# S5 mixer of a two-layer decoder trunk: every block of the gate product from split weights, and a new order of single steps

## The chip, the cores and the metric

The kernel runs on one core of a Trainium2 chip. A core has five engines that work side by side, each through its own instructions in order: TensorE (PE; its weight loads are listed as PEld), VectorE (DVE), ScalarE (ACT), GpSimd (POOL) and SyncE (SP, which here only issues DMAs). TensorE writes its results into PSUM, eight banks of 128 x 512 float32; VectorE and ScalarE read them there. All other tiles lie in SBUF. The metric is the device time of one execution in microseconds (us).

## The reference

A trunk of two layers on 256 rows of width 1024, all in float32. Each layer adds half a SwiGLU block, a mixer, and half a SwiGLU block again; the mixer of layer 0 is an S5 state-space layer, that of layer 1 block attention.

```python
for layer in range(DEPTH):
    h = h + 0.5 * swiglu(rms_norm(h, ...), w_gate, w_up, w_down)
    h = h + mixer(rms_norm(h, mix_norm[layer]))        # S5 in layer 0
    h = h + 0.5 * swiglu(rms_norm(h, ...), w_gate, w_up, w_down)

def s5_mixer(h, ...):
    u = h @ w_in
    y = scan_over_time(lam, B u) @ C + d_skip * u      # 64 groups of 16 channels, 64 states each
    g = gelu(y)
    g = g * sigmoid(g @ w_glu)
    return g @ w_out
```

The change lies in the S5 mixer, in g @ w_glu and in the order of the steps from u = h @ w_in to the first half of g @ w_out. w_in, w_glu and w_out are 1024 x 1024.

## The kernel before

**Products from split weights.** A product that must hold float32 accuracy is made of three products in the type fp32r: a weight w is split into whi, its fp32r rounding (ScalarE), and wlo, the rest w - whi (VectorE), and the other operand likewise; then hi*hi, hi*lo and lo*hi are added up in PSUM (mm3, L398, and L1092 to L1094).

**The stream of weights.** `Stream` (L37) brings all weights of the kernel, in one order, as units of 1 MB into three raw buffers; unit n is loaded when unit n-3 is freed. `split` (L74) splits half a unit: L86 and L87, or L92 and L93 where a norm's gain is multiplied in, each a ScalarE instruction and then a VectorE instruction. Nine pairs of whi and wlo tiles serve as slots; `release` gives one back. `pump` splits the next half if it has been loaded and a slot is free; `get` splits on the spot what a product needs. Freeing a unit issues the next load on SP.

**Blocks left whole.** `add(..., whole=True)` marks a unit that is not split. With WHOLE = 2 this is the first unit of w_glu, which holds the rows of blocks 0 and 1. For these two blocks `glu` multiplies the raw float32 weight with the float32 tile gf (L1090), where other blocks take the three fp32r products. Their unit stays in its raw buffer until the last step of block 1 frees it (L1098).

**The S5 stage** (`s5`, L962). The channels are eight blocks of 128 (b = 0 to 7). The stage is written out as a plan, a string of words, and `step` (L1117) issues one word after the other; that order is the program order on every engine. The words:

- w0, w256, w512 with .t:k are u = h @ w_in for a range of columns, row half t and input block k; with k = 7 ScalarE scales the sum (L999) and VectorE transposes it into U. PSUM tiles pM, two banks in turn.
- t(b): 32 float32 matmuls (L1009) that spread U into the states, in PSUM: banks A0 to A3 for b < 4, then pM in turn. Each issues the load TA of block b+3 on SP.
- r(b): rotation. Two small ScalarE copies (L1020, L1021), six VectorE instructions with two scans (L1028 to L1033), four of POOL (L1035 to L1038, result hr); for b = 1 to 5 the load TE of block b+2.
- y(b): 48 float32 matmuls (L1052) on U and hr with the table TB, then gelu on ScalarE (yg, L1056) and a transpose on VectorE (gs, L1058); the load TB of block b+3.
- g(b): two transposes on TensorE (L1067); then, for blocks that are not whole, ScalarE's fp32r copy (L1070) and VectorE's rest (L1071) into GT, and for all blocks ScalarE's float32 copy gf (L1072). The three read one PSUM bank. GT lies in the buffer ("xa") that the stage's input X used before.
- u(b):o is one step of the gate product g @ w_glu, block b into output block o (`glu`); its sums lie in banks A0 to A3, two output blocks a bank.
- P is a pump; gelu and sigmoid load the ScalarE table ahead of its use; x is the rest of the stage's input.

After the plan, code with loops issues the steps of blocks 6 and 7, each pair of output blocks followed by `gate(i)`, here a(i): a sigmoid of bank Ai on ScalarE (L1103), the multiply on VectorE (L1105), and the split of the result on both (L1107, L1108). Then the first half of the output product follows (`so`, blocks b = 0 and 1 of its four; o(b):q below, with q = 2t + n): it overwrites bank Aq and takes the output of gate b. so(b) needs the weight unit so(b), split in two halves; two pumps stand behind every two steps, one at the end. `boundary` (L373) then makes blocks 2 and 3 with the additions to h (L371) and the preparation of the next SwiGLU.

Units of w_glu and w_out are called glu0 to glu3 and so0 to so3 below, two blocks each.

Of the kernel before, what the change touches and what calls it, by code (L numbers as in the profile page):

```python
# [120 lines left out]
def trunk_kernel(ctx: ExitStack, tc, x, ffn_norm, ffn_w_gate, ffn_w_up, ffn_w_down, mix_norm,  # L121
# [32 lines left out]

    units = []
    where = {}
    WHOLE = 2
    GAIN = {"f00": None, "f01": 8, "f10": 16, "f11": 24, "s5": 32, "moba": 40}

    def add(key, load, gains=None, whole=False):  # L160
# [118 lines left out]
    st = Stream(nc, units, rp, hp)  # L279
# [20 lines left out]
    XP = [xp]  # L300
# [661 lines left out]
    def s5(nxt, entry):  # L962
        V, P = nc.vector, nc.gpsimd
        HALVES = (slice(0, 64), slice(64, 128))
        wstack = ExitStack()
# [108 lines left out]
        def glu(b, os):  # L1074

            u = where["glu", b // 2]
            g = gf[b // 2][:, b % 2, :]
            if b < WHOLE:
                w = st.raw[u][:, b % 2 * 1024:b % 2 * 1024 + 1024]
            else:  # L1080
                gh, gl = GT["h"][:, b, :], GT["l"][:, b, :]
                wh, wl = st.get(u, b % 2)
            for o in os:
                first, last = b == 0 and o % 2 == 0, b == NB - 1
                if first:
                    acc[o // 2] = psA(o // 2)
                d = acc[o // 2][:, (o % 2) * 256:(o % 2) * 256 + 256]
                c = slice(o * 128, o * 128 + 128)
                if b < WHOLE:
                    mm(d, w[:, c], g, start=first, stop=last, skip_group_check=True)  # L1090
                else:
                    mm(d, wh[:, c], gh, start=first, stop=False, skip_group_check=True)  # L1092
                    mm(d, wh[:, c], gl, start=False, stop=False, skip_group_check=True)
                    mm(d, wl[:, c], gh, start=False, stop=last, skip_group_check=True)  # L1094
                if o == 7 and b >= WHOLE:
                    st.release(u, b % 2)
                elif o == 7 and b % 2:
                    st.free_raw(u)  # L1098

        def gate(i):  # L1100

            sg = fp.tile([128, 2, 256], F32, name="sg", tag="gr", bufs=2)
            nc.scalar.activation(sg, acc[i].rearrange("p (a c) -> p a c", a=2), AF.Sigmoid)  # L1103
            g = gf[i]
            V.tensor_tensor(g, g, sg, op=OP.mult)  # L1105
            gh, gl = (GT[p][:, 2 * i:2 * i + 2, :] for p in "hl")
            nc.scalar.activation(gh, g, AF.Copy)  # L1107
            V.tensor_tensor(gl, g, gh.bitcast(F32), op=OP.subtract)  # L1108
# [8 lines left out]
        def step(word):  # L1117
            name, _, ks = word.partition(":")
            ks = [int(k) for k in ks.split("-")] if ks else []
            ks = range(ks[0], ks[-1] + 1) if ks else ()  # L1120
            if name[0] == "w":
                c0, t = name[1:].split(".")
                for k in ks:
                    w_in(int(c0), int(t), k)
            elif name[0] == "u":
                glu(int(name[1]), ks)
            elif name == "x":
                if entry:
# [8 lines left out]
        plan = """
            w0.0:0-1 P x w0.0:2-5 P w0.0:6 w0.1:0 w0.0:7 w0.1:1-4 P w0.1:5-7 w256.0:0-4 w256.1:0-1 t0 w256.0:5  # L1140
            w256.1:2 P w256.0:6 r0 w256.1:3 w256.0:7 P t1 w512.0:0 w256.1:4-7 w512.0:1 r1 w512.0:2-3 t2 gelu
            r2 t3 y0 w512.0:4-5 w512.1:0-1 w512.0:6 w512.1:2 r3 w512.1:3-4 w512.0:7 w512.1:5 y1 w512.1:6-7 g0
            y2 P P u0:0-1 g1 t4 u0:2-3 r4 g2 u0:4 t5 u0:5-7 r5 u1:0 t6 y3 u1:1-2 r6 u1:3-7 u2:0-2 t7 y4 g3
            u2:3-5 r7 y5 u2:6-7 u3:0-2 y6 g4 u3:3-4 g5 u3:5-7 P u4:0 P u4:1 P u4:2 g6 y7 u4:3-4 P P u4:5-7
            u5:0-1 sigmoid g7 u5:2-5 P u5:6-7 P
        """
        for word in plan.split():
            step(word)
        wstack.close()
        lstack.close()  # L1150
        XP[0] = xstack.enter_context(tc.tile_pool(name="xt2", bufs=1))
        for i in range(4):
            glu(6, (2 * i, 2 * i + 1))
            glu(7, (2 * i, 2 * i + 1))
            gate(i)
        for b in range(2):
            for t in range(2):
                for n in range(2):
# [316 lines left out]
```

## Time and profile before

| | |
|---|---|
| median of 3 runs | 982.28 us (981.8 to 982.3) |
| the profiled execution's own time | 982.36 us |
| its span in the trace | 980.4 us |
| first product of the S5 stage (L399 into pM) | 213.48 us |
| first product of o0 | 287.14 us |
| first product of the SwiGLU behind (L553) | 310.77 us |
| DVE / ACT / POOL busy in the span | 70% / 57% / 19% |
| granted clock of TensorE | 0.999 |

Times in a timeline are from the span's start. A row gives start, duration, engine, source line, operation, output <- input, shape, count of merged instructions, and in brackets the idle time ahead with what ended it. TensorE's matmuls are pipelined, so a row's duration includes the pipeline's depth, and what an instruction costs is read from one start to the next. A wait for several semaphores is put down to the one that came last.

### The profile page before, as it was taken

What the parts mean: (1) busy time and instruction counts of PE and PEld (TensorE: products, weight loads), DVE (VectorE), ACT (ScalarE), POOL (GpSimd) and SP (SyncE); (2) the same over time, 40 slices, a digit from 0 to 9 for tenths busy, and PEclk for the clock granted to TensorE, in tenths of its full rate; (3) what the DMA queues carried; (4) which work ended last, traced back from release to release, by engine and by line L of the source; (5) the groups of instructions that cost most, each with busy time, mean ns of one, the idle gap of its engine ahead of it and who ended that gap; (6) DMA issues with size and microseconds to landing.
All of it is one profiled execution on the core that took longest, in us unless ns stands there. A gap on an engine that the chain in (4) does not pass through costs nothing.

```text
span 980.4 us, 17231 instructions
## 1 busy us (share of the span) xinstructions
PE 972.2 (99%) x6727; PEld 867.5 (88%) x6727; DVE 688.8 (70%) x1118; ACT 560.4 (57%) x1008; POOL 186.5 (19%) x364
## 2 busy tenths in 40 slices
PE   9999999999999999999999999999999999999998
PEld 7878888788888999999999999998788899999997
DVE  5799767768768676666667766665789667766662
ACT  7565766553267555555456655544897556655540
POOL 6963544416511000000010000000441010000000
PEclk9999999999999999999999999999999999999999
DMA  8988877887645666565536656562544546656531
GB/s 284 249 269 279 275 261 242 298 324 245 252 173 182 213 208 215 172 212 175 172 125 214 221 173 214 173 215 92 172 145 157 186 143 214 231 174 213 172 130 44
DMA packets 140002, 198.74 MB, mean 203 GB/s; under 512 B 18232, under 2 KB 111504, under 8 KB 139664
## 3 DMA queue, kind: packets, MB, share of 16 engines
q1 hardware_dynamic: 133808, 184.32, 57.5%
q0 software_dynamic: 5536, 12.71, 3.6%
q8 instruction: 53, 0.87, 0.4%
q10 hardware_dynamic: 576, 0.61, 0.3%
q14 instruction: 29, 0.24, 0.1%
HBM read 183.89 MB, written 13.66 MB: 202 GB/s over the span
## 4 chain that ended last, share of the span: by engine, by line
PE 94%; DVE 2%; ACT 2%; issue 1%; POOL 1%; DMA 1%; SPq 0%; POOLq 0%; DVEq 0%; ACTq 0%
PE pM L554 13%; PE pM L553 13%; PE pM L555 13%; PE pA L399 9%; PE pA L401 9%; PE pA L400 9%; PE pM L399 6%; PE pM L400 6%; PE pM L401 6%; PE pA L473 1%; PE pR L1052 1%; PE pR L333 1%; DVE wlo L87 1%; PE pA L1090 1%; PE pR L866 1%
## 5 line engine op out<-in xcount | busy, mean ns | idle before, releaser
L553 PE MATMUL pM<-xa,whi 128*128 128x256 f32 x1056 | 295.7, 280 | 0.0
L554 PE MATMUL pM<-xa,whi 128*128 128x256 f32 x1056 | 294.9, 279 | 0.0
L555 PE MATMUL pM<-xa,wlo 128*128 128x256 f32 x1056 | 294.7, 279 | 0.0
L93 DVE SCALAR_TENSOR_TENSOR wlo<-raw,gT,whi 128x512 fp32r<-128x512 f32 x328 | 228.1, 748 | 71.2 <-ACT whi L92 71.0
L87 DVE TENSOR_TENSOR wlo<-raw,whi 128x1024 fp32r<-128x1024 f32 (+1 forms) x155 | 187.5, 1225 | 56.0 <-ACT whi L86 54.8
L92 ACT ACTIVATE whi<-raw,gT 128x512 fp32r<-128x512 f32 x328 | 213.7, 711 | 16.4 <-PE pA L401 14.6
L554 PEld LDWEIGHTS pM<-xa,whi 128*128 128x128 f32 x1056 | 198.5, 188 | 2.6
L553 PEld LDWEIGHTS pM<-xa,whi 128*128 128x128 f32 x1056 | 198.5, 188 | 2.3
L555 PEld LDWEIGHTS pM<-xa,wlo 128*128 128x128 f32 x1056 | 198.5, 188 | 0.0
L86 ACT ACTIVATE whi<-raw 128x1024 fp32r<-128x1024 f32 (+1 forms) x155 | 158.7, 1049 | 26.1 <-DMA raw<-in_ffn_w_up_dram 9.8
L399 PE MATMUL pA<-whi,ah 128*128 128x512 f32 x352 | 138.8, 394 | 0.0
L400 PE MATMUL pA<-wlo,ah 128*128 128x512 f32 x352 | 137.6, 391 | 0.0
L401 PE MATMUL pA<-whi,al 128*128 128x512 f32 x352 | 137.6, 391 | 0.0
L568 ACT ACTIVATE sg<-gr 128x256 f32<-128x256 f32 x66 | 27.6, 418 | 165.7 <-DVE gr L565 165.7
L399 PE MATMUL pM<-whi,xa 128*128 128x512 f32 (+1 forms) x304 | 122.2, 402 | 0.0
L400 PE MATMUL pM<-wlo,xa 128*128 128x512 f32 (+1 forms) x304 | 115.8, 381 | 0.1
L401 PE MATMUL pM<-whi,xa 128*128 128x512 f32 (+1 forms) x304 | 115.5, 380 | 0.0
L348 POOL TENSOR_TENSOR ms<-ss 128x1 f32<-128x1 f32 x10 | 1.9, 193 | 470.3 <-ACT sq L345 470.3
L401 PEld LDWEIGHTS pA<-whi,al 128*128 128x128 f32 x352 | 66.1, 188 | 14.3
L399 PEld LDWEIGHTS pA<-whi,ah 128*128 128x128 f32 x352 | 66.1, 188 | 11.6
L400 PEld LDWEIGHTS pA<-wlo,ah 128*128 128x128 f32 x352 | 66.2, 188 | 11.3
L565 DVE TENSOR_TENSOR gr<-pM,rrow 128x512 f32<-128x512 f32 x66 | 45.5, 689 | 40.9 <-PE pM L555 40.8
(269 smaller groups left out, 1214.5 us busy)
## 6 DMA issues: line engine op xcount, KB each, us to landing
raw<-in_ffn_w_down_dram SPq DMA_DIRECT2D x44, 1024.0 KB, 5.4
raw<-in_ffn_w_gate_dram SPq DMA_DIRECT2D x80, 512.0 KB, 4.0
raw<-in_ffn_w_up_dram SPq DMA_DIRECT2D x80, 512.0 KB, 5.1
raw<-in_moba_w_qkv_dram SPq DMA_DIRECT2D x12, 1024.0 KB, 5.1
TB<-dB SPq DMA_DIRECT2D x8, 768.0 KB, 6.6
raw<-in_ffn_w_gate_dram SPq DMA_DIRECT2D x16, 256.0 KB, 4.4
raw<-in_ffn_w_up_dram SPq DMA_DIRECT2D x16, 256.0 KB, 4.7
dB<-tt POOLq DMA_DIRECT2D x16, 256.0 KB, 5.1
```

The source lines that it names most:

```text
L86: nc.scalar.activation(hi[:, c], r[:, c], AF.Copy)
L87: nc.vector.tensor_tensor(lo[:, c], r[:, c], hi[:, c].bitcast(F32), op=OP.subtract)
L92: nc.scalar.activation(hi[:, c], r[:, c], AF.Identity, scale=g)
L93: nc.vector.scalar_tensor_tensor(lo[:, c], r[:, c], g, hi[:, c].bitcast(F32), op0=OP.mult, op1=OP.subtract)
L399: mm(o, xh, wh, start=start, stop=False)
L400: mm(o, xh, wl, start=False, stop=False)
L401: mm(o, xl, wh, start=False, stop=stop)
L553: mm(o, a, xh, start=k == 0 and i == 0, stop=False, skip_group_check=True)
L554: mm(o, a, xl, start=False, stop=False, skip_group_check=True)
L555: mm(o, b, xh, start=False, stop=k == 7, skip_group_check=True)
L565: V.tensor_tensor(gr, ps.rearrange("p (i c) -> p i c", i=2), Rr["row"][:, None, :].to_broadcast([128, 2, 256]), op=OP.mult)
L568: nc.scalar.activation(sg, gr[:, 0, :], AF.Silu)
```

## The change

WHOLE becomes 0, so no unit is left whole: glu0 is split in two halves like the others, blocks 0 and 1 of the gate product are made of three fp32r products, and GT is laid out at g(0) instead of g(2). The plan now also holds the steps of blocks 6 and 7, the gates (words a0 to a3) and the first half of the output product (words o0, o1), which the loops issued before; inside it the order of steps and of pumps is new.

```diff
-    WHOLE = 2
+    WHOLE = 0
...
+            elif name[0] == "a":
+                if name == "a0":
+                    wstack.close()
+                    lstack.close()
+                    XP[0] = xstack.enter_context(tc.tile_pool(name="xt2", bufs=1))
+                gate(int(name[1]))
+            elif name[0] == "o":
+                b = int(name[1])
+                for k in ks:
+                    so(b, k // 2, k % 2)
+                    if k == 3:
+                        for i in range(2):
+                            st.release(where["so", b], i)
...
         plan = """
-            w0.0:0-1 P x w0.0:2-5 P w0.0:6 w0.1:0 w0.0:7 w0.1:1-4 P w0.1:5-7 w256.0:0-4 w256.1:0-1 t0 w256.0:5
-            w256.1:2 P w256.0:6 r0 w256.1:3 w256.0:7 P t1 w512.0:0 w256.1:4-7 w512.0:1 r1 w512.0:2-3 t2 gelu
-            r2 t3 y0 w512.0:4-5 w512.1:0-1 w512.0:6 w512.1:2 r3 w512.1:3-4 w512.0:7 w512.1:5 y1 w512.1:6-7 g0
-            y2 P P u0:0-1 g1 t4 u0:2-3 r4 g2 u0:4 t5 u0:5-7 r5 u1:0 t6 y3 u1:1-2 r6 u1:3-7 u2:0-2 t7 y4 g3
-            u2:3-5 r7 y5 u2:6-7 u3:0-2 y6 g4 u3:3-4 g5 u3:5-7 P u4:0 P u4:1 P u4:2 g6 y7 u4:3-4 P P u4:5-7
-            u5:0-1 sigmoid g7 u5:2-5 P u5:6-7 P
+            w0.0:0-1 P x w0.0:2-5 P w0.0:6 w0.1:0 w0.0:7 w0.1:1-5 w256.0:0-1 w0.1:6 P w256.0:2 w0.1:7
+            w256.0:3-4 w256.1:0-2 t0 w256.1:3-4 P r0 w256.1:5 w256.0:5-6 gelu w256.1:6 w256.0:7 t1 w512.0:0 r1
+            w256.1:7 w512.0:1-2 w512.1:0 w512.0:3 P w512.1:1-3 t2 w512.0:4-5 r2 y0 t3 r3 w512.1:4 w512.0:6-7
+            w512.1:5-6 y1 g0 w512.1:7 y2 P u0:0 P u0:1-2 g1 u0:3 g2 u0:4 t4 t5 u0:5 P r4 u0:6-7 y3 u1:0-2 r5
+            u1:3-4 t6 u1:5-7 g3 u2:0-3 r6 u2:4 t7 y4 r7 u2:5-7 y5 g4 u3:0 P u3:1-2 y6 u3:3-4 g5 u3:5-7 u4:0-2
+            P P P g6 u4:3-7 u5:0 y7 u5:1-3 P u5:4-5 g7 u5:6 P u5:7 u6:0 sigmoid u6:1 u7:0-1 a0 u6:2-3 P u7:2-3
+            a1 u6:4-5 u7:4-5 P a2 u6:6-7 u7:6-7 a3 o0:0-1 P P o0:2-3 P P o1:0-1 P P o1:2-3 P
         """
         for word in plan.split():
             step(word)
-        wstack.close()
-        lstack.close()
-        XP[0] = xstack.enter_context(tc.tile_pool(name="xt2", bufs=1))
-        for i in range(4):
-            glu(6, (2 * i, 2 * i + 1))
-            glu(7, (2 * i, 2 * i + 1))
-            gate(i)
-        for b in range(2):
-            for t in range(2):
-                for n in range(2):
-                    so(b, t, n)
-                if t == 1:
-                    for i in range(2):
-                        st.release(where["so", b], i)
-                st.pump(2 - b * t)
```

## The prediction

> **What bounds the kernel now.** I read the page first, then the S5 stage (213 to 311 us) by stretches, then the timeline of each engine there.
>
> ```profile
> PE 972.2 (99%) x6727; PEld 867.5 (88%) x6727; DVE 688.8 (70%) x1118; ACT 560.4 (57%) x1008; POOL 186.5 (19%) x364
> ```
>
> ```profile
> 262.00:282.00 20.00, 18.88 (x288) 17.76 (x282) 12.79 (x21) 11.12 (x22) 7.66 (x9) 1.00 0.60 224
> ```
>
> TensorE is busy for 99% of the span. In 262 to 282 us (columns: length, then busy time of PE, weight load, DVE, ACT, POOL, then clock) it has the stage's largest hole, 1.1 us, at full clock, and VectorE works 12.8 of 20 us. So a TensorE saving counts at once, and so does any lateness of VectorE that outgrows its idle third. These are the TensorE rows I price with:
>
> ```profile
> 241.42 0.34 PE L1052 MATMUL pR<-U,TB 128*64 128x64 f32 x4
> ...
> 242.97 0.50 PE L399 MATMUL pM<-whi,xa 128*128 128x512 f32 x1
> 243.31 0.40 PE L400 MATMUL pM<-wlo,xa 128*128 128x512 f32 x1
> ...
> 244.79 0.34 PE L1052 MATMUL pR<-U,TB 128*64 128x64 f32 x4
> ...
> 253.82 1.15 PE L1009 MATMUL pM<-U,TA 128*64 128x63 f32 x32 [0.33 <-issue]
> 254.77 0.32 PE L1052 MATMUL pR<-U,TB 128*64 128x64 f32 x4
> ...
> 256.30 3.29 PE L1090 MATMUL pA<-gf,raw 128*128 128x256 f32 x14
> ...
> 267.98 0.34 PE L1052 MATMUL pR<-U,TB 128*64 128x64 f32 x4
> ...
> 270.51 0.38 PE L1067 MATMUL pR<-cst,gs 128*128 128x128 f32 x2
> 270.85 0.28 PE L1093 MATMUL pA<-xa,whi 128*128 128x256 f32 x1
> ...
> 278.55 0.41 PE L1067 MATMUL pR<-cst,gs 128*128 128x128 f32 x2 [1.12 <-DVE gs L1058]
> ...
> 282.35 0.28 PE L1094 MATMUL pA<-xa,wlo 128*128 128x256 f32 x1
> 286.91 0.28 PE L1094 MATMUL pA<-xa,wlo 128*128 128x256 f32 x1
> ...
> 288.20 0.40 PE L399 MATMUL pA<-whi,xa 128*128 128x512 f32 x1
> 298.57 0.39 PE L399 MATMUL pA<-whi,xa 128*128 128x512 f32 x1
> ```
>
> Start to start, 39 products of 256 columns take 4.56 us, 0.117 each, so one split gate step (three products) is 0.351. 45 of 512 columns take 10.37, 0.23 each. A y step takes 1.55 to the next product, which is itself 0.11 late (0.34 for 0.23): 1.66. A t step is 0.95, and the way back from it to products 0.23 (1.55 less 48 matmuls at 0.95/32, plus the 0.11). A g step is 0.34 less one product: 0.22.
>
> **The change, part by part.**
>
> *TensorE's work.* Sixteen float32 steps go (seven are the 14 records at 256.30: at most 3.29/7 = 0.47 each; at least 0.42 if the last record's pipeline tail is left out) and sixteen at 0.351 come: -1.1 to -1.9 us, say -1.6. Counting the plan's words, products follow a t or y step 11 times instead of 6; five more returns at 0.23 and entries of some 0.1 are +1.6, from which the changes into and out of float32 that vanish come off (the rows merge them; between 0 and -1.6; I take the middle). Net -0.8, bounds -1.9 to +0.5. The holes of 0.33 (t6) and 1.12 (g7) are there to be won as well.
>
> *VectorE's and ScalarE's work.* Added: two splits of glu unit 0 and, for blocks 0 and 1, the fp32r copy (L1070) and its rest (L1071). L1072's copy reads the same PSUM bank after L1071, so ScalarE, in order, now waits for VectorE in g0 and g1 too; behind g1's wait stand g2's copies, the next split and rotation 4's preparation. The rows that price this:
>
> ```profile
> 246.88 0.45 DVE L1058 STREAM_TRANSPOSE gs<-yg 128x256 f32<-128x256 f32 x1 [0.76 <-ACT yg L1056]
> 247.82 2.36 DVE L87 TENSOR_TENSOR wlo<-raw,whi 128x1024 fp32r<-128x1024 f32 x2 [0.50 <-ACT whi L86]
> 250.10 0.68 DVE L1028 TENSOR_TENSOR wv<-pM,TE 128x512 f32<-128x512 f32 x1
> ...
> 253.63 0.40 DVE L1071 TENSOR_TENSOR xa<-pR,xa 128x256 fp32r<-128x256 f32 x1
> 254.55 0.69 DVE L1028 TENSOR_TENSOR wv<-pM,TE 128x512 f32<-128x512 f32 x1 [0.52 <-ACT pM L1020]
> ...
> 260.77 1.26 DVE L1033 TENSOR_TENSOR_SCAN zo<-rh,pM 128x256 f32<-128x256 f32 x2
> ...
> 270.44 0.40 DVE L1071 TENSOR_TENSOR xa<-pR,xa 128x256 fp32r<-128x256 f32 x1
> 271.57 0.42 DVE L1071 TENSOR_TENSOR xa<-pR,xa 128x256 fp32r<-128x256 f32 x1 [0.73 <-ACT xa L1070]
> 273.40 3.50 DVE L87 TENSOR_TENSOR wlo<-raw,whi 128x1024 fp32r<-128x1024 f32 x3 [1.40 <-ACT whi L86]
> ...
> 265.33 0.74 POOL L1038 TENSOR_TENSOR hr<-pv,pv 128x256 f32<-128x256 f32 x1
> ```
>
> *Up to y2: nothing.* Ahead of y2 stand the same words in both plans (all w, t0 to t3, y0, y1, g0), so I leave y2 at 244.8.
>
> ```profile
> 240.93 0.74 POOL L1038 TENSOR_TENSOR hr<-pv,pv 128x256 f32<-128x256 f32 x1
> ```
>
> A split of glu unit 0 now stands between rotations 1 and 2, 1.2 us (2.1 beside POOL, below). Today POOL is through with rotation 2 at 241.7, y2 needs it at 244.8: 3.1 us of TensorE's steps cover it. Without that cover it would cost its 1.2 to 2.1.
>
> *Rotation 4, then t6.* Today gs2, two subtracts (247.82) and rotation 4 at 250.10. New order: gs2, two subtracts, rest of g1, rest of g2, a third subtract, rotation 4. The pattern rest, rest, subtract stands at 270.44, 271.57, 273.40: 2.96 us, because of ScalarE's hops. Rotation 4 starts at 250.1 + 2.96 + 1.17 = 254.2, ends (3.53, 250.10 to 253.63) at 257.8. t6 takes over t4's PSUM bank and waits for that: 257.95. TensorE is ready earlier: y2 and y3 3.32, 13 gate steps 4.56, g1 and g2 0.44, t4 and t5 2.13: 10.5 behind 244.8, 255.3. **Wait 2.6.**
>
> *Rotation 6, then y6.* 257.8, a transpose 0.4, rotation 5 to 261.7, a rest with its hop 0.92 (253.63 to 254.55), rotation 6 from 262.6 to 266.1; POOL needs 4.05 more (scan's end 262.03 to 266.07): y6 at 270.3, today 267.98. TensorE's own work from t6: t6 and t7 2.36, y4 and y5 3.32, 14 gate steps 4.91, g3 and g4 0.44: 269.0. **Wait 1.3.**
>
> *Up to g7.* 266.1, transpose and rotation 7 to 270.05, transpose, rest of g4 at 270.45; subtract of glu2's first half 1.83 later (271.57 to 273.40), 272.3. POOL is still at rotation 7 then. The one subtract that ran beside POOL's SBUF products:
>
> ```profile
> 227.80 2.09 DVE L87 TENSOR_TENSOR wlo<-raw,whi 128x1024 fp32r<-128x1024 f32 x1
> ...
> 228.77 2.17 POOL L1036 TENSOR_TENSOR pv<-zo,TE 128x512 f32<-128x512 f32 x1
> ```
>
> 2.09 instead of 1.17 (POOL's usual is 1.19): bounds 1.17 and 2.09, I take the latter. Then gs6 and the rest of g5 at 274.8; from there the same chain as today (that rest at 271.57, three splits, rest of g6, gs7) leads to g7 6.98 later: 281.7. TensorE's own work gives 280.9 (today's 9.45 from y6 to the hole before g7, less g4, plus four gate steps).
>
> The Trainium skill ("GPSIMD Engine Reference", 1. Specifications) says that GpSimd shares its SBUF interfaces with VectorE and contends with instructions that have two SBUF inputs. The 2.09 agrees with it, and by it two more splits (glu0's first, glu2's first) run at that price; by a plain 1.17 the end comes 0.8 earlier, 985.7.
>
> *The gates.* The splits of so1 move from ahead of all gates to between them.
>
> ```profile
> 279.83 1.28 ACT L234 ACT_TABLE_LOAD   x1
> ...
> 284.27 0.59 ACT L1103 ACTIVATE sg<-pA 128x512 f32<-128x512 f32 x1
> 286.45 0.63 ACT L1107 ACTIVATE xa<-gf 128x512 fp32r<-128x512 f32 x1 [1.59 <-DVE gf L1105]
> ...
> 285.74 0.68 DVE L1105 TENSOR_TENSOR gf<-gf,sg 128x512 f32<-128x512 f32 x1
> ...
> 287.73 0.68 DVE L1105 TENSOR_TENSOR gf<-gf,sg 128x512 f32<-128x512 f32 x1
> ...
> 291.71 0.68 DVE L1105 TENSOR_TENSOR gf<-gf,sg 128x512 f32<-128x512 f32 x1
> ...
> 294.05 4.63 DVE L87 TENSOR_TENSOR wlo<-raw,whi 128x1024 fp32r<-128x1024 f32 x4 [0.26 <-ACT whi L86]
> ...
> 302.88 0.69 DVE L371 SCALAR_TENSOR_TENSOR h<-pA,h 128x512 f32<-128x512 f32 x1 [0.22 <-PE pA L401]
> ```
>
> Behind g7: the subtract of so0's first half, the rest of g7, copy, the next split, the table load, sigmoid 0: its multiply about 5.2 us after g7, 286.9 (an estimate: subtract with hop 1.5, rest 0.45, copy 0.3, split 0.95, table 1.4, sigmoid 0.6). A gate takes 1.99 from multiply to multiply (285.74, 287.73); with a split behind it, 2.34 to the subtract (291.71 to 294.05) plus 1.17: 3.5. Multiplies at 286.9, 290.4, 293.9. Sigmoid 2 starts 0.71 (285.74 to 286.45) + 0.54 + 0.95 behind multiply 1, ends 293.2; o0:2 overwrites the bank that it reads. TensorE, 281.7 + 0.22 + 18 gate steps + 0.3 (for g7's rest) + 12 products, is there at 291.3: **wait 1.9.** Sigmoid 3 ends at 295.8, **wait 1.2** for o0:3. The 30 products left (o0:3 and o1) end at 302.7; today the products behind them begin at 298.57: **+4.1.**
>
> *Boundary.* The last multiply, 295.9, plus today's 11.2 (291.71 to 302.88) frees VectorE at 307.1; TensorE needs the first sum at 302.7 + 4.31 = 307.0. +0.1; bounds 0 and +1 if the next phase's first load lands later behind its subtract.
>
> *Queues.* SP issues in program order: glu3's megabyte moves ahead of TA7, so0's ahead of TE6, TB6, TE7. I cost that at nothing (rival 4). gelu's table load (1.3) moves ahead of t1, where ScalarE waits for products; if not, it costs 1.3 once. g0 takes over the s5 input's buffer while the last w step has yet to read block 7; g0 writes block 0, so I cost no wait (rival 3).
>
> Sum: 982.36 (the profiled run; the median shown is 982.28) + 4.2 = **986.5 us**; its own range 985.2 to 988.
>
> **The rivals.** 1. *VectorE keeps pace* (the other side). Place: rotation 4 to y6 and the gates. For it: the 7 us idle in 262 to 282, more than the 3.2 added (two subtracts 2.34, two rests 0.8). Against: the order puts the additions ahead of rotation 4. It decides where rotation 4 starts before 251.6 and sigmoid 2 ends before TensorE is at o0:2. Then -0.8 - 0.33 - 1.12: 980.1. 2. *Only the gates wait*, the rotations keep up: 980.1 plus 1.5 for each of the two splits between gates less the 0.3: 982.8. For it: the gates' order is in the plan itself, and the rotations' lateness hangs on ScalarE's hops; against: rotation 4 has three subtracts ahead of it however the hops fall. 3. *A wait for the old buffer*: the last w step waits for g0's copies, about 1.1 (the hop 270.44 to 271.57), carried to the end: 987.6. For it: one buffer, two tiles; against: other blocks. 4. *SP's queue*: so0's load waits for glu1's second subtract (254.2), and TE6 stands behind its issue, say at 254.8.
>
> ```profile
> TE<-dE SPq DMA_DIRECT2D x8, 260.0 KB, 4.5
> ...
> raw<-in_s_w_in_dram SPq DMA_DIRECT2D x1, 1024.0 KB, 14.0
> ```
>
> At 4.5 us TE6 lands at 259.3, rotation 6 needs it at 262.6: 3.3 us of slack, against which stands that a load has taken 14. Half way between, 9.25, it lands at 264.05 and costs 1.5: 988.0.
>
> **How the numbers follow.** Forecast 0.58, rival 1 0.13, rival 2 0.13, rival 3 0.08, rival 4 0.08. About 0.2% (2 us) can be told from no change: faster is below 980.3, slower above 984.2. Faster: rival 1, most of it, 0.13. Same: rival 2, 0.13. Slower: the rest, 0.74. The range leaves out rival 1 and a little above: 981.5 to 988.8.
>
> **What would show it.** No L1090 rows; a hole of about 2.6 us ahead of t6 (L1009), released by VectorE's scan, and 1.3 ahead of y6, released by POOL; rotation 4 near 254; subtracts of about 2 us beside L1035 and L1036; multiplies of L1105 3.5 apart where a split lies between; two holes in the first so products. I am wrong if t6 runs on without a hole, or if the sigmoids stay 2 us apart.

## The result, and the profile after

| | before | after |
|---|---|---|
| median of 6 executions each | 982.28 us (981.8 to 982.86) | 987.31 us (985.8 to 987.91) |
| ratio | | 1.0049 [1.0038, 1.0061] |
| span of the profiled execution | 980.4 us | 985.9 us |
| granted clock of TensorE in the six executions of after | | 0.998, 0.998, 0.998, 0.998, 0.997, 1.0 |

The changed kernel is 5.0 us slower; 986.5 had been forecast. The sixth execution, the only one with the full clock, took 985.8 us. The profiled execution took 987.91 us.

In the trace of after the stage begins 0.74 us later than in that of before, with the same code ahead of it: the rest of the stage's input (L336), at 214.39 us then, stands at 215.13 now. Forecast times below are moved by this 0.74. VectorE's timeline of after (start, duration, engine, line, operation; in brackets the idle time ahead and what ended it):

```profile
215.13 0.69 DVE L336 TENSOR_TENSOR xa<-pR,xa 128x512 fp32r<-128x512 f32 x1 [0.37 <-ACT xa L335]
...
251.32 0.42 DVE L1071 TENSOR_TENSOR xa<-pR,xa 128x256 fp32r<-128x256 f32 x1
252.47 0.42 DVE L1071 TENSOR_TENSOR xa<-pR,xa 128x256 fp32r<-128x256 f32 x1 [0.72 <-ACT xa L1070]
254.29 1.23 DVE L87 TENSOR_TENSOR wlo<-raw,whi 128x1024 fp32r<-128x1024 f32 x1 [1.40 <-ACT whi L86]
255.43 0.68 DVE L1028 TENSOR_TENSOR wv<-pM,TE 128x512 f32<-128x512 f32 x1
...
263.73 0.42 DVE L1071 TENSOR_TENSOR xa<-pR,xa 128x256 fp32r<-128x256 f32 x1 [0.82 <-ACT xa L1070]
264.67 0.69 DVE L1028 TENSOR_TENSOR wv<-pM,TE 128x512 f32<-128x512 f32 x1 [0.52 <-ACT pM L1020]
...
274.20 1.57 DVE L87 TENSOR_TENSOR wlo<-raw,whi 128x1024 fp32r<-128x1024 f32 x1 [1.40 <-ACT whi L86]
...
288.29 0.69 DVE L1105 TENSOR_TENSOR gf<-gf,sg 128x512 f32<-128x512 f32 x1 [0.78 <-ACT sg L1103]
...
291.77 0.68 DVE L1105 TENSOR_TENSOR gf<-gf,sg 128x512 f32<-128x512 f32 x1
...
295.24 0.69 DVE L1105 TENSOR_TENSOR gf<-gf,sg 128x512 f32<-128x512 f32 x1
```

The first block is the forecast pattern word for word: rest, rest, third subtract, and then rotation 4 at 255.43. The multiplies of the gates stand 3.48 apart where a split lies between. TensorE's timeline of after, its rows with idle time, and the first product behind the stage:

```profile
259.15 1.98 PE L1009 MATMUL pM<-U,TA 128*64 128x63 f32 x32 [2.50 <-issue]
...
272.32 0.34 PE L1052 MATMUL pR<-hr,TB 128*64 128x64 f32 x4 [0.18 <-POOL hr L1038]
...
282.98 0.41 PE L1067 MATMUL pR<-cst,gs 128*128 128x128 f32 x2
...
294.60 0.50 PE L399 MATMUL pA<-whi,xa 128*128 128x512 f32 x1 [1.62 <-ACT sg L1103]
297.13 0.50 PE L399 MATMUL pA<-whi,xa 128*128 128x512 f32 x1 [0.86 <-ACT sg L1103]
316.25 0.37 PE L553 MATMUL pM<-xa,whi 128*128 128x256 f32 x1
```

Holes, times in which TensorE is idle, of 2.50 us ahead of t6, 1.62 ahead of o0:2 and 0.86 ahead of o0:3; in y6 next to none (0.18). g7 no longer waits. But t6's 32 matmuls, 1.15 us long before, take 1.98. The busy time by stretches of after says why (length, then busy time of PE, weight load, DVE, ACT, POOL with instruction counts, then granted clock, DMA share, GB/s):

```profile
256.00:258.00 2.00, 0.65 (x6) 0.45 (x4) 1.80 (x5) 0.00 (x0) 0.00 (x0) 1.00 0.71 166
...
259.00:260.00 1.00, 0.84 (x16) 0.88 (x18) 1.00 (x4) 0.00 (x0) 0.81 (x1) 0.57 0.99 379
260.00:261.00 1.00, 1.00 (x22) 0.94 (x18) 0.97 (x2) 0.00 (x0) 1.00 (x2) 0.50 1.19 453
261.00:262.00 1.00, 1.00 (x7) 0.94 (x5) 0.83 (x3) 0.00 (x0) 0.92 (x2) 0.50 0.97 402
262.00:263.00 1.00, 1.00 (x8) 1.00 (x7) 0.91 (x2) 0.00 (x0) 1.00 (x2) 0.72 0.52 185
```

Behind the hole the granted clock falls to half for some 3.4 us. Compared with the full clock, these four microseconds lack 0.43 + 0.50 + 0.50 + 0.28 = 1.7 us of work.

The loss adds up on TensorE. From L336 to the first L553 the stage takes 96.38 us before (214.39 to 310.77) and 101.12 after: 4.74 more. Holes go from 0.33 + 1.12 to 2.50 + 0.18 + 1.62 + 0.86 = 5.16, 3.7 more; the half clock is 1.7; the rest, -0.7, is TensorE's own work, a remainder that was not measured by itself.

### The profile page after: what moved, and what is told of

It is laid out like the page before. It is cut to its first block, busy times and chain, and to the rows that moved or that the text cites. A ratio compares the mean times of both kernels' runs of the same rounds, so it can differ in the third digit from the quotient of the medians.

```text
span 985.9 us, 17272 instructions
## 1 busy us (share of the span) xinstructions
PE 973.3 (99%) x6743; PEld 868.9 (88%) x6743; DVE 693.1 (70%) x1122; ACT 563.5 (57%) x1012; POOL 186.3 (19%) x364
## 4 chain that ended last, share of the span: by engine, by line
PE 87%; DVE 5%; ACT 2%; issue 2%; POOL 2%; DMA 1%; SPq 0%; DVEq 0%; POOLq 0%; ACTq 0%
PE pM L554 13%; PE pM L553 13%; PE pM L555 12%; PE pA L399 9%; PE pA L401 9%; PE pA L400 9%; PE pM L399 5%; PE pM L400 5%; PE pM L401 5%; DVE wlo L87 2%; PE pA L473 1%; ACT whi L86 1%; PE pR L333 1%; POOL qrs L306 1%; PE pR L866 1%
## 5 line engine op out<-in xcount | busy, mean ns | idle before, releaser
L553 PE MATMUL pM<-xa,whi 128*128 128x256 f32 x1056 | 295.7, 280 | 0.0
L555 PE MATMUL pM<-xa,wlo 128*128 128x256 f32 x1056 | 294.6, 279 | 0.0
L87 DVE TENSOR_TENSOR wlo<-raw,whi 128x1024 fp32r<-128x1024 f32 (+1 forms) x157 | 190.7, 1229 | 59.1 <-ACT whi L86 57.9
L553 PEld LDWEIGHTS pM<-xa,whi 128*128 128x128 f32 x1056 | 198.5, 188 | 2.3
L86 ACT ACTIVATE whi<-raw 128x1024 fp32r<-128x1024 f32 (+1 forms) x157 | 161.2, 1049 | 27.1 <-DMA raw<-in_ffn_w_up_dram 9.8
L399 PE MATMUL pA<-whi,ah 128*128 128x512 f32 x352 | 138.8, 394 | 0.0
L401 PE MATMUL pA<-whi,al 128*128 128x512 f32 x352 | 137.6, 391 | 0.0
L399 PE MATMUL pM<-whi,xa 128*128 128x512 f32 (+1 forms) x304 | 122.3, 402 | 0.0
L401 PE MATMUL pM<-whi,xa 128*128 128x512 f32 (+1 forms) x304 | 115.4, 380 | 0.0
L401 PEld LDWEIGHTS pA<-whi,al 128*128 128x128 f32 x352 | 66.1, 188 | 14.3
L399 PEld LDWEIGHTS pA<-whi,ah 128*128 128x128 f32 x352 | 66.1, 188 | 11.6
```

What stands on the lines that cost most here:

```text
L86: nc.scalar.activation(hi[:, c], r[:, c], AF.Copy)
L87: nc.vector.tensor_tensor(lo[:, c], r[:, c], hi[:, c].bitcast(F32), op=OP.subtract)
L399: mm(o, xh, wh, start=start, stop=False)
L401: mm(o, xl, wh, start=False, stop=stop)
L553: mm(o, a, xh, start=k == 0 and i == 0, stop=False, skip_group_check=True)
L555: mm(o, b, xh, start=False, stop=k == 7, skip_group_check=True)
```

## The experiments

Time before is the median of the runs of before on the same chip as each group: 982.63 us for the first four, 982.86 for the next four, 982.73 for the last two. The stage is the time from L336 to the first L553 in the run's trace; before has 96.38 us, after 101.12. Two runs of different groups are better compared by it than by their medians.

| run | median, us | ratio to before | stage, us |
|---|---|---|---|
| third_split_later | 985.86 | 1.0034 [1.0022, 1.0047] | 99.39 |
| gates_free | 988.04 | 1.0055 [1.0041, 1.0069] | 101.95 |
| new_plan_whole2 | 985.61 | 1.0031 [1.0019, 1.0042] | 99.39 |
| filler | 986.3 | 1.0038 [1.0025, 1.0051] | 100.31 |
| gates_only | 983.88 | 1.0011 [1.0002, 1.002] | 97.09 |
| old_order_split | 984.6 | 1.0022 [1.0013, 1.0031] | 97.66 |
| best_order_split | 983.63 | 1.0008 [0.9999, 1.0017] | 96.87 |
| best_order_whole2 | 978.27 | 0.9955 [0.9942, 0.9967] | 92.23 |
| best_order_split2 | 978.92 | 0.9962 [0.9949, 0.9974] | 92.20 |
| split2_order_whole2 | 982.71 | 1.0002 [0.9993, 1.0011] | 96.05 |

**third_split_later.** The changed kernel with one pump moved behind rotation 5.

```diff
-            w512.1:5-6 y1 g0 w512.1:7 y2 P u0:0 P u0:1-2 g1 u0:3 g2 u0:4 t4 t5 u0:5 P r4 u0:6-7 y3 u1:0-2 r5
+            w512.1:5-6 y1 g0 w512.1:7 y2 P u0:0 P u0:1-2 g1 u0:3 g2 u0:4 t4 t5 u0:5 r4 u0:6-7 y3 u1:0-2 r5 P
```

> Changed against the new kernel: the split of glu1's second half stands behind rotation 5 instead of ahead of rotation 4. Theory A (VectorE's whole queue up to rotation 6 is the limit, wherever in it the split stands): rotation 4 starts about 2 us earlier and the hole ahead of t6 shrinks from 2.5 to 0.5 us, so the clock is not throttled behind it; but y6, which waits for rotation 6, starts at most 1 us earlier and gets a hole of about 2 us. Time 986.0 (985.4 to 986.6). Rival B (the hole ahead of t6 costs its own length, and the throttled clock on top): y6 3 to 4 us earlier, time 983.7. Rival C (the throttled clock costs nothing because VectorE is the limit either way): time 987.3 as the new kernel, y6 where it was.

985.86 us: theory A. TensorE's timeline, rows with idle time:

```profile
257.25 1.15 PE L1009 MATMUL pM<-U,TA 128*64 128x63 f32 x32 [0.50 <-issue]
...
270.02 0.34 PE L1052 MATMUL pR<-hr,TB 128*64 128x64 f32 x4 [0.99 <-POOL hr L1037]
270.70 0.34 PE L1052 MATMUL pR<-hr,TB 128*64 128x64 f32 x4 [0.35 <-POOL hr L1038]
```

The hole ahead of t6 falls from 2.50 to 0.50 and t6 takes its 1.15 us again, at full clock. The later rotations become the new wait: y5 and y6 wait for the halves of hr that POOL makes, 0.2 + 0.99 + 0.35 us, where after had 0.18. So of the 2.0 us of hole and 1.7 of clock that are won at t6, 1.4 come back in these waits and 0.6 in places where no wait shows; the stage is 1.7 us shorter, the median 1.45.

**filler.** Ten idle products of the helper `busy` ahead of t6, in a word b10 of the plan; they compute nothing that is used.

```diff
+            elif name[0] == "b":
+                busy(int(name[1:]))
...
-            u1:3-4 t6 u1:5-7 g3 u2:0-3 r6 u2:4 t7 y4 r7 u2:5-7 y5 g4 u3:0 P u3:1-2 y6 u3:3-4 g5 u3:5-7 u4:0-2
+            u1:3-4 b10 t6 u1:5-7 g3 u2:0-3 r6 u2:4 t7 y4 r7 u2:5-7 y5 g4 u3:0 P u3:1-2 y6 u3:3-4 g5 u3:5-7 u4:0-2
```

> Changed against the new kernel: ten float32 products of 128 columns of ones into a spare PSUM tile just ahead of t6, so that TensorE is not idle there; their result is not used. Theory A (the hole lets the clock be throttled to half for some 3 us; by that g3's transposes, the rest of g3 and rotation 6 come late): clock 1.000 in every run, steps of 0.117 behind t6, a hole of about 1.2 us ahead of y6; time 985.8 (985.4 to 986.3), the time of the one run of the new kernel whose clock was 1.000. Rival C (VectorE's queue sets y6 either way): 987.3, y6 where it was.

986.3 us, the upper end of theory A's range: filling the hole with useless work makes the kernel 1.0 us faster. TensorE's timeline:

```profile
256.48 2.40 PE L1370 MATMUL pR<-ones 128*128 128x128 f32 x20
259.14 1.15 PE L1009 MATMUL pM<-U,TA 128*64 128x63 f32 x32 [0.27 <-issue]
```

t6 starts where it started (259.15), but takes 1.15 us instead of 1.98: the time of the hole isn't won, only the clock. Of the 1.7 us, 0.4 come back as longer waits for hr: 0.54 (0.18 in after), where 1.2 had been expected.

**gates_free.** The two splits of so1 stand behind the last gate.

```diff
-            P P P g6 u4:3-7 u5:0 y7 u5:1-3 P u5:4-5 g7 u5:6 P u5:7 u6:0 sigmoid u6:1 u7:0-1 a0 u6:2-3 P u7:2-3
-            a1 u6:4-5 u7:4-5 P a2 u6:6-7 u7:6-7 a3 o0:0-1 P P o0:2-3 P P o1:0-1 P P o1:2-3 P
+            P P P g6 u4:3-7 u5:0 y7 u5:1-3 P u5:4-5 g7 u5:6 P u5:7 u6:0 sigmoid u6:1 u7:0-1 a0 u6:2-3 u7:2-3
+            a1 u6:4-5 u7:4-5 a2 u6:6-7 u7:6-7 a3 P P o0:0-1 P P o0:2-3 P P o1:0-1 P P o1:2-3 P
```

> Changed against the new kernel: the two splits of so1 stand behind the four gates instead of between them. Both theories: the gates' multiplies 2.0 us apart, no hole ahead of o0:2 and o0:3. Theory A (a backlog of VectorE: the splits have to be done before o1 anyway): the holes come back ahead of o1, whose weights are late, about 2 us of the 2.5; time 986.8 (986.3 to 987.2). Rival B (the place between the gates is what costs): the two holes of 1.6 and 0.9 us are won, time 984.8.

988.04 us: no gain, and more than either theory had. The multiplies are 2.0 apart now, and the holes ahead of o0 are gone, but the waits of TensorE name new ones (engine, tile, line <- what: total us, times, longest):

```profile
PE pA L399 <- ACT whi L86: 0.8, 1, 0.8
PE pA L400 <- DVE wlo L87: 0.8, 1, 0.8
```

These are the halves of so1, late for o1. The profiled execution was at half clock behind its hole of 2.50 ahead of t6, too, and fell to half once more behind the two new holes (the clock is the third figure from the end):

```profile
299.00:300.00 1.00, 1.00 (x3) 0.50 (x2) 1.00 (x2) 1.00 (x2) 0.00 (x0) 0.50 0.00 0
300.00:301.00 1.00, 1.00 (x4) 0.78 (x3) 1.00 (x2) 1.00 (x2) 0.00 (x0) 0.50 0.34 49
301.00:302.00 1.00, 1.00 (x4) 0.81 (x3) 1.00 (x2) 0.72 (x1) 0.00 (x0) 0.50 1.02 351
```

With 0.87 and 0.93 in the microseconds at both ends that is 1.7 us again, more than the 0.9 by which the holes behind g7 are shorter (1.58 for 2.48). So this run shows that the splits are late for o1 when they are moved, but not what the gates would gain at full clock; its one execution with a clock of 1.0 took 987.62, and why it is no faster stays open.

**new_plan_whole2.** The new plan with blocks 0 and 1 in float32: the order without the added work.

```diff
-    WHOLE = 0
+    WHOLE = 2
```

> The new order of steps, but blocks 0 and 1 of the gate product in float32 from the raw weight as before. Theory A (the order and the added work share the loss): ahead of rotation 4 the three subtracts stay, the two rests with their hops go, so rotation 4 starts 2 to 3 us earlier, t6's hole is under 0.8 us, no throttled clock; every later split is two halves ahead. Time 984.7 (984.0 to 985.5). Rival B (the added work alone): 982.3, as the old kernel. Rival C (the order alone): 987.3, as the new one.

985.61 us, 0.1 above the range of theory A, by which order and added work share the loss; B and C are further off. VectorE's timeline and TensorE's largest wait:

```profile
286.16 0.69 DVE L1105 TENSOR_TENSOR gf<-gf,sg 128x512 f32<-128x512 f32 x1 [0.78 <-ACT sg L1103]
...
295.10 0.69 DVE L1105 TENSOR_TENSOR gf<-gf,sg 128x512 f32<-128x512 f32 x1
```

```profile
PE pA L399 <- ACT sg L1103: 2.5, 2, 1.6
```

t6 has next to no hole here (0.15 us) and the clock stays at 1.00. The first multiply is 0.4 us later than before (285.74) and the last 3.4 (291.71); as the stage begins 0.4 later in this trace, the first stands where it stood, and the last is 3.0 late. So 3.0 us of the change come with the order alone (the stage has 99.39 for 96.38), most of them as the two holes ahead of o0:2 and o0:3, and 1.7 (99.39 to 101.12) with the added work. That is no more than the half clock behind t6's hole takes, which this run doesn't have; filler, at full clock but with the hole's time still lost, lies 0.9 above this run.

**gates_only.** The kernel of before with the two splits of so1 between the gates, all else untouched.

```diff
-            u5:0-1 sigmoid g7 u5:2-5 P u5:6-7 P
+            u5:0-1 sigmoid g7 u5:2-7
...
             glu(6, (2 * i, 2 * i + 1))
+            if i in (1, 2):
+                st.pump()
             glu(7, (2 * i, 2 * i + 1))
```

> The kernel of before with one part of the change alone: the two splits of so1 leave the plan's last line and stand behind glu(6) of the second and of the third gate. All else is as before. Theory A (a split between two gates delays the next multiply): in the trace of before the multiplies of L1105 stand at 285.74, 287.73, 289.72, 291.71, and the first waits for the two subtracts of 283.46; without them it follows the sigmoid, which ends at 284.9, so it comes 0.8 earlier. Then two spacings of 3.5 (measured in the changed kernel: 288.29, 291.77, 295.24) and one of 2.0: the last multiply at 293.95, 2.2 later than before. TensorE, which is at o0:2 at 290.95, waits for sigmoids 2 and 3 (291.25 and 293.8): 0.3 and 1.2, 1.5 together. Time before plus 1.5 to 2.2: 983.8 to 984.6 us, multiplies 3.5 apart. Theory B (the gates have room for a split in the 0.70 that VectorE waits for ScalarE in each): no later than before, 981.8 to 982.6.

983.88 us, 1.0 more than before: the mechanism is A's, the size is less. VectorE's timeline:

```profile
284.34 0.69 DVE L1105 TENSOR_TENSOR gf<-gf,sg 128x512 f32<-128x512 f32 x1 [1.58 <-ACT sg L1103]
...
287.83 0.69 DVE L1105 TENSOR_TENSOR gf<-gf,sg 128x512 f32<-128x512 f32 x1
...
291.31 0.68 DVE L1105 TENSOR_TENSOR gf<-gf,sg 128x512 f32<-128x512 f32 x1
293.30 0.68 DVE L1105 TENSOR_TENSOR gf<-gf,sg 128x512 f32<-128x512 f32 x1
```

The spacings are 3.49, 3.48 and 1.99 as expected; but the first multiply comes 2.1 us earlier (this trace runs 0.7 late), where 0.8 were expected, since ScalarE's part of the two splits had held up the sigmoid as well (it starts at 284.27 before, right behind them, and at 283.71 here). A split between gates costs little if the work taken from ahead of the gates lets the first one start earlier. In the changed kernel it didn't: g7 came late, and a subtract of so0 (286.29) still stood ahead of the first multiply (288.29).

**old_order_split.** The old plan and gate section with WHOLE = 0, two pumps more.

```diff
-    WHOLE = 2
+    WHOLE = 0
...
-            y2 P P u0:0-1 g1 t4 u0:2-3 r4 g2 u0:4 t5 u0:5-7 r5 u1:0 t6 y3 u1:1-2 r6 u1:3-7 u2:0-2 t7 y4 g3
-            u2:3-5 r7 y5 u2:6-7 u3:0-2 y6 g4 u3:3-4 g5 u3:5-7 P u4:0 P u4:1 P u4:2 g6 y7 u4:3-4 P P u4:5-7
+            y2 P P u0:0-1 g1 t4 u0:2-3 r4 g2 u0:4 t5 u0:5-7 r5 u1:0 t6 y3 u1:1-2 r6 u1:3-7 P u2:0-2 t7 y4 g3
+            u2:3-5 r7 y5 u2:6-7 P u3:0-2 y6 g4 u3:3-4 g5 u3:5-7 P u4:0 P u4:1 P u4:2 g6 y7 u4:3-4 P P u4:5-7
```

> The old plan and the old gate section with WHOLE = 0: all products from split weights, with the two subtracts more that this needs ahead of u2:0 and ahead of u3:0 (the two subtracts behind y2 now split glu unit 0). It is the added work without the new order. Theory A (the order made the loss, the added work can be carried): rotation 4 has the same two subtracts ahead of it as before, and the rest of g0 and of g1 besides, of which that of g1 comes with its hop directly ahead, 0.42 + 0.73; so about 1.1 more than the 0.33 of before at t6. Two subtracts of 1.17 more up to g7, of which the idle time of VectorE in 262 to 282 covers none to all: 0 to 2.3. TensorE's products save 1.1 to 1.9 there. Between 981.5 and 984.2, about 983. Theory B (VectorE's work is the bound wherever it stands): its added work of 2 x 1.17 + 2 x 0.42 = 3.2 and the hops of the two rests, 2 x 0.73, come out whole: 986 to 987. Theory C (the new order was needed for the added work, and is the better home for it): later than the changed kernel, over 987.5.

984.6 us, 1.7 more than before. That lies between A and B, 0.4 above A's range. TensorE's waits:

```profile
PE pM L1009 <- issue: 2.3, 1, 2.3
PE pR L1067 <- DVE gs L1058: 1.7, 1, 1.7
```

The holes are those that the kernel before has already, grown: t6's from 0.33 to 2.25, g7's from 1.12 to 1.70. The trace's stage is 1.3 us longer than before's, at full clock. Six of the eleven executions have a clock of 0.999 or 1.0 and took 984.06 to 984.6; the five at 0.998 took 985.35 to 986.2, so part of the median's 1.7 may be the clock, though no trace shows where. So the loss is a sum: 1.3 to 1.7 for the work, about 3 for the order. Theory C is out: the new order was no better home for it.

**best_order_split and best_order_whole2.** Two plans laid out anew, one for WHOLE = 0, one for WHOLE = 2; of each the part from y1 to the gates:

```diff
+            w512.1:5-6 r3 w512.0:4 w512.1:7 y1 g0 w512.0:5-6 g1 w512.0:7 P y2 t4 r4 u0:0 t5 y3 g2 u0:1-2
+            u1:0-2 u0:3 t6 u1:3 r5 u0:4 g3 u2:0 r6 u0:5 u2:1 y4 t7 u0:6 u3:0 u0:7 u2:2-3 u1:4-5 u3:1-2 u2:4
+            u3:3 r7 P y5 g4 y6 u3:4 u1:6 P u2:5 u3:5 P u4:0-1 u1:7 y7 g5 u4:2 g6 u4:3-4 u5:0 g7 u5:1 P u5:2
+            u2:6 u4:5 P u6:0 P u5:3-4 u2:7 P u6:1-4 u7:0-2 P P u5:5 u3:6 u6:5 u4:6 u7:3 u5:6 sigmoid u3:7
+            u4:7 u6:6 u7:4-5 a0 u5:7 u7:6 a1 a2 u6:7 u7:7 a3 P o0:0-2 P o0:3 o1:0 P P o1:1-3 P P
...
-    WHOLE = 0
+    WHOLE = 2
...
+            w512.1:2-3 r3 w512.0:7 w512.1:4-6 P w512.1:7 u0:0 y1 y2 t4 r4 t5 y3 r5 u0:1-2 g1 g2 u0:3-4 u1:0
+            t6 u1:1-4 u0:5 u1:5 u0:6-7 r6 y4 t7 r7 y5 u1:6-7 g3 g4 u2:0-5 u3:0-1 u2:6 g5 P u4:0 u3:2 y6 P
+            y7 u3:3 u4:1 u2:7 P u5:0 u4:2 g6 g7 u5:1 P u3:4 u5:2 u4:3 u6:0 u5:3 P u4:4 u3:5 u4:5 u7:0 u6:1
+            u5:4 P u6:2 u7:1 sigmoid u5:5 u3:6 u7:2 a0 u4:6 u5:6 u6:3-4 u7:3 u3:7 u4:7 u6:5 u7:4-5 u5:7
+            u6:6 a1 u6:7 P u7:6-7 a2 a3 o0:0-2 P o0:3 P o1:0 P o1:1 P P o1:2-3
```

> The changed kernel (WHOLE = 0, all work of it) with its plan in another order: two subtracts fewer stand ahead of rotation 4 (only one, behind g1, ahead of y2), g2's and g3's rests come behind rotations 4 and 5, t6 stands behind u0 to u1:2, products of u0 to u3 are kept back as cover for the rotations, both splits of so1 stand ahead of the first gate, and the last three gates follow each other with few words between. Theory A (the loss is the order's, the work fits): no hole over 1 us ahead of t6, y6 and g7, and no hole of 1 us in the first output products; what is left is TensorE's saving of 0.8 and the 0.33 and 1.12 of old holes: 980 to 982 us. Theory B (VectorE's added 3.2 us is a backlog that any order carries to the gates): the first multiply of L1105 comes 2 to 3 us later than before, and the time is 984 to 986.

983.63 us, between the theories. It avoids the holes that were forecast for the change and has others. Three single waits, in the timelines of ScalarE, TensorE and VectorE:

```profile
245.75 0.39 ACT L1070 ACTIVATE xa<-pR 128x256 fp32r<-128x256 f32 x1 [2.29 <-PE pM L401]
```

```profile
247.06 0.34 PE L1052 MATMUL pR<-U,TB 128*64 128x64 f32 x4 [1.35 <-ACT gf L1072]
```

```profile
261.28 0.69 DVE L1028 TENSOR_TENSOR wv<-pM,TE 128x512 f32<-128x512 f32 x1 [1.36 <-DMA TE<-dE]
```

g0's copy writes into the buffer that the last w steps read, and waits for the last of them, 2.29 us; y2 needs the bank and waits with it. And rotation 6 waits for its table, whose load was issued behind so0's. The second is rival 4's wait. The first is at rival 3's buffer, but runs the other way: rival 3 let the last w step wait for g0's copies.

> The same step function with a plan laid out anew in the same way, but with blocks 0 and 1 in float32 as before (WHOLE = 2): no work added, order alone. Theory A (the order of before had 0.33 and 1.12 us of holes and VectorE bound the boundary behind the gates; an order can win them): 979 to 981 us, without holes over 0.5 us ahead of t6, y6 and g7. Theory B (TensorE's own work is the bound and the old order already hid all but those holes, each plan has its own returns to pay): 981.5 to 983. If this kernel is faster than best_order_split by 1 us or more, split weights for blocks 0 and 1 are not worth their VectorE work under any of the orders tried; if the two are alike, the choice of weights matters less than the order.

978.27 us, faster than before by 4.6, a little beyond theory A. TensorE's only wait in the stage:

```profile
PE pR L1052 <- POOL hr L1038: 0.3, 1, 0.3
```

Rotations 4 to 7 (247.46 to 260.43 us) run without a split's subtract between them, the next one is at 268.68, and but for one at 284.12 all that so1 needs lie ahead of the gates. So the old order itself left 4.6 us (4.15 of them in the stage), of which only 1.45 showed as holes in its trace. By the measure set beforehand this run, 5.4 us below best_order_split, spoke against the split weights; the next one takes that back.

**best_order_split2 and split2_order_whole2.** One more plan for WHOLE = 0, without the three waits above, and the same plan with WHOLE = 2.

```diff
+            w0.0:0-1 P x w0.0:2-5 P w0.1:0-4 w0.0:6-7 w0.1:5 P w0.1:6 w256.0:0 w0.1:7 w256.0:1 P w256.0:2 P
+            w256.0:3-5 w256.1:0 w256.0:6 w256.1:1 w256.0:7 w256.1:2-3 t0 w256.1:4-5 P w256.1:6 P P w256.1:7
+            t1 w512.0:0 w512.1:0 r0 w512.1:1-3 gelu r1 w512.1:4 t2 w512.1:5 r2 w512.0:1 w512.1:6-7 t3 y0
+            w512.0:2 r3 w512.0:3-7 y1 g0 t4 r4 y2 t5 g1 u0:0 r5 u0:1 y3 u1:0 u0:2 g2 u0:3-4 u1:1-2 u0:5 t6
+            t7 r6 y4 u2:0 g3 u1:3 u2:1 u0:6 u1:4 u2:2-4 r7 y5 g4 u1:5 u3:0-2 y6 g5 u0:7 u3:3 g6 u1:6 u2:5
+            u3:4 u2:6 P u1:7 P y7 u3:5 u2:7 P u4:0-2 u5:0 sigmoid g7 u5:1-2 u6:0 u4:3 P u5:3 P u3:6 u6:1 P
+            u6:2 u4:4 u5:4 u4:5 u7:0-1 u6:3 P P u4:6 u7:2 a0 u6:4 u7:3 P u7:4 u5:5 P u3:7 a1 u5:6 u4:7
+            u6:5-6 u7:5-6 u5:7 u6:7 a2 u7:7 a3 o0:0-3 o1:0-2 P P P P P o1:3
```

> The changed kernel (WHOLE = 0) with one more order, made against what the trace of best_order_split shows: there g0's copy waited for the last w step (y2 behind it 1.35 us late, t4 0.86), and rotation 6 waited 1.36 us for its table, issued behind the load of so0 (y6 behind it 1.3 late). Here g0 stands behind all w steps, rotation 4 follows t4 with no subtract ahead of it but those long done, and the splits of glu 1 to so1 stand behind rotation 7. Theory A (the added work can be carried whole, what is lost in an order are such single waits): the 983.63 of best_order_split less 1.35 + 0.86 and most of 1.3: 980 to 981.5. Theory B (VectorE's added 3.2 us stays as a backlog behind rotation 7 and comes out at the gates in any order): first multiply of L1105 again 1 us or more later than before's 285.74, 983 to 985.

978.92 us: theory A, and faster than its range. All work of the changed kernel is in it, and TensorE has no wait in the stage. VectorE's timeline and one stretch:

```profile
246.92 0.69 DVE L1028 TENSOR_TENSOR wv<-pM,TE 128x512 f32<-128x512 f32 x1 [0.52 <-ACT pM L1020]
...
251.71 0.69 DVE L1028 TENSOR_TENSOR wv<-pM,TE 128x512 f32<-128x512 f32 x1 [0.52 <-ACT pM L1020]
...
256.50 0.69 DVE L1028 TENSOR_TENSOR wv<-pM,TE 128x512 f32<-128x512 f32 x1 [0.52 <-ACT pM L1020]
...
261.30 0.69 DVE L1028 TENSOR_TENSOR wv<-pM,TE 128x512 f32<-128x512 f32 x1 [0.52 <-ACT pM L1020]
...
269.93 2.36 DVE L87 TENSOR_TENSOR wlo<-raw,whi 128x1024 fp32r<-128x1024 f32 x2 [1.40 <-ACT whi L86]
...
281.65 0.68 DVE L1105 TENSOR_TENSOR gf<-gf,sg 128x512 f32<-128x512 f32 x1
...
299.07 0.69 DVE L371 SCALAR_TENSOR_TENSOR h<-pA,h 128x512 f32<-128x512 f32 x1 [3.04 <-PE pA L401]
```

```profile
240.00:256.00 16.00, 16.00 (x308) 14.44 (x308) 13.79 (x27) 4.55 (x14) 12.59 (x15) 1.00 0.86 285
```

Rotation 4 is at 246.92 instead of 255.43, and the four follow each other in 4.8 us with one rest between; no split comes between them. Four subtracts of glu 0 and 1 lie ahead, at 223 to 229 us, where TensorE has w steps; eight lie behind rotation 7. VectorE is busy 13.8 of 16 us in 240 to 256, in after 10.7: the same work, earlier. The first multiply is at 281.65, 4.1 us ahead of before's, and at the boundary it is VectorE that waits for TensorE (3.04 us).

> The order of best_order_split2 with blocks 0 and 1 in float32 (WHOLE = 2): the same order without the added work; the two splits that it doesn't need are done earlier for later units. The pair prices the added work within one order, as the pairs before/old_order_split (1.7) and new_plan_whole2/changed kernel (1.7) do within theirs. Theory A (that price is 1.5 to 2 us in any order, because VectorE has no spare time near the gates): 1.5 to 2 us below best_order_split2. Theory B (in an order laid out for it the added work is covered, and TensorE's saving of 0.8 shows): 0.5 to 1 us above best_order_split2.

982.71 us: neither theory, 3.8 above its twin. Timelines of ScalarE and of TensorE:

```profile
224.79 1.06 ACT L86 ACTIVATE whi<-raw 128x1024 fp32r<-128x1024 f32 x1 [2.03 <-DMA raw<-in_s_w_glu_dram]
...
228.95 2.00 ACT L86 ACTIVATE whi<-raw 128x1024 fp32r<-128x1024 f32 x2 [1.79 <-DMA raw<-in_s_w_glu_dram]
```

```profile
231.37 0.50 PE L399 MATMUL pM<-whi,xa 128*128 128x512 f32 x1 [1.88 <-ACT us L999]
```

With unit glu0 whole, the early pumps split later units, and these haven't landed: ScalarE waits 2.03 and 1.79 us for their loads, the scaling of the w sums (L999) waits behind it, and TensorE 1.88 behind that and 0.54 once more. So this pair doesn't price VectorE's added work; it shows that a plan fits the units that it was laid out for. The remaining 1.4 of the 3.8 are TensorE's own work, added up in the way of the next paragraph: 0.7 in the steps u, 0.55 in the transposes of g, 0.25 in the w and o products, and 0.1 less in t and y.

**The gate product itself.** Adding up, from TensorE's timelines, the time from each start to the next (a hole counts to the row ahead of it) gives for the steps u, split and whole together, and for the w and o products from the stage's first product on:

| | before | after | old_order_split | best_order_whole2 | best_order_split2 | split2_order_whole2 |
|---|---|---|---|---|---|---|
| steps u, us | 27.50 | 28.43 | 28.83 | 24.85 | 24.01 | 24.71 |
| w and o0 to so3 products (L399 to L401), us | 46.09 | 49.14 | 45.89 | 45.17 | 45.70 | 47.83 |
| L336 to first L553, us | 96.38 | 101.12 | 97.66 | 92.23 | 92.20 | 96.05 |

Between the two plans with next to no holes, best_order_whole2 (0.35 us) and best_order_split2 (none), the steps u differ by 0.84 us for the split weights, and the rest by 0.8 against them, 0.53 of it in the w and o products; the stages are equal to 0.03 us, and 978.27 and 978.92 lie 0.07% apart. The two plans differ in more than the weights; within one plan, best_order_split2's, the steps u are 0.7 us shorter with split weights.

## Why the prediction was right

The time (986.5 for 987.31) and the sign are right, and so is the mechanism, VectorE's lateness at rotation 4 and at the gates. That the number is so near is in part luck: a loss that the prediction doesn't have, the half clock, stands in for waits that didn't come, and its times are too short for TensorE's own work.

- **TensorE's work, -0.8.** The sum over the stage leaves -0.7. Right as a term; the forecast's times don't keep to it (see the sum).
- **Up to y2, nothing.** y2 at 245.85, forecast 245.54. Right to 0.3 us; g0's copy did wait 0.67 us for the last w step, and VectorE's rest (L1071) behind it, but TensorE didn't.
- **Rotation 4, then t6.** Forecast 254.9 and a hole of 2.6; measured 255.43 and 2.50, and third_split_later shows that the third subtract is what does it: moved, the hole is 0.50.
- **Rotation 6, then y6.** Forecast a hole of 1.3 and y6 at 271.0. y6 starts at 271.69 and waits only 0.18. This is the step that was off: TensorE's own work from t6 to y6 was taken at full clock, and ran at half for 3.4 us, 1.7 us more. TensorE was late itself, and so hardly waited. filler shows the two apart: with the clock held, the waits for hr are 0.54, still less than half of the 1.3, and the kernel is 1.0 faster.
- **Up to g7.** Forecast 282.4, measured 282.98, but not for the forecast's reason: its times leave TensorE a wait of 0.8 there (281.7 against 280.9), and TensorE came without one, just after VectorE's transpose, which ended at 282.84. The subtracts beside POOL's products took 2.17 (at 232.72 us) and 1.57 (at 274.20) where 2.09 was taken. What the Trainium skill says of the shared interfaces ("GPSIMD Engine Reference", 1. Specifications) agrees with both being longer than 1.17.
- **The gates.** Forecast multiplies at 287.6, 291.1, 294.6; measured 288.29, 291.77, 295.24: 3.48 apart for 3.5. Holes 1.9 and 1.2 forecast, 1.62 and 0.86 measured. new_plan_whole2 has the same two holes (1.63 and 0.88) without the added work, so they are the order's.
- **The sum.** Forecast holes 2.6 + 1.3 + 1.9 + 1.2 = 7.0, and 7.8 with the 0.8 ahead of g7; measured holes 5.16 and clock 1.7, 6.9. From y2 to the first product of so2 (244.79 to 298.57 before) the forecast's times, 244.8 to 302.7, leave TensorE 50.1 us of work, 2.2 less than before and not 0.8. In after (245.85 to 304.08) it is 51.3 without holes and lost clock, 0.9 less than before. So 0.9 us too much of loss and 1.2 too little of work nearly cancel.
- **The rivals.** 1 and 2 fell: VectorE didn't keep pace at rotation 4, though best_order_split2 shows that with all the added work it can. 3 and 4 didn't occur in the changed kernel: TE6 was issued at 256.02, right behind so0's load at 255.54, and rotation 6 at 264.67 didn't wait for it. In best_order_split rival 4's wait came, where rotation 6 was earlier, and at rival 3's buffer the opposite wait, of g0's copy for the last w step.

What the prediction didn't divide is the loss: it let all of it come from VectorE's lateness. The runs put 1.7 us down to the added work (1.3 to 1.7 in the old order) and about 3 to the order, and show in best_order_split2 that neither had to be.

## What to carry to other kernels

A chain that runs through a side engine (here VectorE's six instructions and POOL's four for each rotation) should have nothing between its links that could be done before or behind it, even where the engine is a third idle on the mean. Before a change of method is blamed, run the new method in the old order and the old method in the new one: here the method cost 1.3 to 1.7 us and the order 3 in these plans, and in two plans with next to no holes the methods came out equal and some 4 us faster than before. An order is laid out for one method: the best plan for the split weights cost the other 3.8 us.

## What the runs showed of the hardware that wasn't expected

A single hole of 2.50 us in TensorE's work was followed by a granted clock of 0.50, for about 3.4 us in all; with a hole of 0.50 instead (third_split_later) or with products in it (filler) the clock stayed up. The mean clock of five of the six executions of the changed kernel has it (0.997 or 0.998); the sixth, at 1.0, was 1.5 us below the median. In gates_free the same 2.50 us were followed by the half clock only from 261 us on, 1.5 us after TensorE had resumed, and there a second slow stretch, as long, followed two holes of only 0.82 and 0.76 us, with one product of 0.50 us between them. Yet in the traced execution of after the holes of 1.62 and 0.86 us ahead of o0 left the clock at 1.00, as did a hole of 2.25 us in that of old_order_split, while five of that kernel's eleven executions have 0.998. So the length of a hole doesn't decide by itself.

The Trainium skill ("TensorE: Matmul & The Clock Gate", Part 1, What's actually happening) has the clock set by an activity window of 3413 ns that runs freely. The length of the three slow stretches and their changing start agree with that, but the holes that sufficed here are shorter than the idle window of some 3.4 us that the page asks for. What decides beyond a hole's length wasn't tried.
